# Weight sums of a Strassen down projection: from the down stage to the merge stage, by way of DRAM

## The chip, the cores and the metric

The kernel runs on one core of a Trainium2 chip. A core has five engines that each work through their own list of instructions in order: TensorE (PE, matmuls; PEld is its weight load), VectorE (DVE), ScalarE (ACT), GpSimd (POOL) and SyncE (SP, which here only issues transfers). They wait for each other by semaphores. Transfers are issued by SyncE or GpSimd and done by 16 DMA engines. The metric is the device time of one execution in microseconds; lower is better.

## The reference

A decoder block on x of 1024 tokens by 1024 channels, in float32. Two branches read the same normed input, each is projected to 1024 channels and gated, then follow an output projection and a SwiGLU feed-forward part. What matters here is the merge of the branches and the end:

```python
h = rms_norm(x, norm1_g[l])
z = jnp.einsum('bsd,dn->bsn', h, w_in[l])
...                                    # y_nsa, y_ret: 1024 tokens x 512 each
u = jnp.einsum('nbsc,ncd->bsnd', jnp.stack([y_nsa, y_ret]), w_branch[l])
gates = jax.nn.sigmoid(zm.reshape(b, s, N_BRANCH, D_MODEL))
mixed = jnp.sum(gates * u, axis=2)
x = x + jnp.einsum('bsd,de->bse', mixed, w_out[l])
h = rms_norm(x, norm2_g[l])
ff = jax.nn.silu(h @ ffn_w_gate[l]) * (h @ ffn_w_up[l])     # 1024 x 2816
x = x + ff @ ffn_w_down[l]                                  # w_down: 2816 x 1024
```

## The kernel before

**Products.** A float32 product is made of three passes of TensorE: both operands are split into a high half (ScalarE rounds it to the matmul format) and a low half (VectorE subtracts the high half), and high x high, high x low and low x high are summed in one PSUM bank. So each operand tile costs one ScalarE and one VectorE instruction, `split()`.

**Order.** The Python program doesn't write the engines' lists directly. Generators (streams) yield operations, and a planner (`Sched`, L113 to L208) picks at each step the operation that by its own cost estimates can begin first; for equal begin the priority decides (a lower number first). What it picks is fixed at build time as each engine's order; on the chip an engine never goes past an instruction that waits. An operation given as `Any` (`both()`, L1708) goes to VectorE or GpSimd, whichever the planner expects to end first. Tiles come from rings: `Alloc` takes the next slot of a ring once the one before in it is released.

**The merge stage** (L1228 to L1311). For each of 8 column blocks c there is one branch unit "u" (`w_branch`) and, for c = 0, 1 and 7, two gate units "z" (for c = 2 to 6 the gates were made earlier and come back from `z_scr`). A unit's weights come into `wraw` and are split into `wh`, from a ring of two slots (`hl_ring`, L364). A branch unit is four groups of 12 matmuls, for branch b = 1, 0 and token half 0, 1, each in one of the four PSUM banks "SSSO" (`psS` three times, `psO`). The stream `merge_out` empties a bank: for b = 1 VectorE writes gate x bank into `mx`; for b = 0 it multiplies in place in `sgm` and adds this to `mx`. The branches' outputs y lie in DRAM. `y_loads` brings them in 16 tiles of 128x512 through a ring `yraw` of four slots, and `y_split` splits them into `yt`, in the order b = 1, 0, half 0, 1, k = 0 to 3. Then follow the output projection (`wo`), the norm, and gate and up, which write F in DRAM (`f_scr`).

**The down stage** (L1693 to L1940). F times `w_down` is cut into 2x2 blocks A (of F) and B (of `w_down`), each block into 11 slices k of 128x512 (KH = 11), and done in 7 products instead of 8. With the sums

```
S1 = A21 + A22    S2 = S1 - A11    A22 - A11    A12 - S2
T1 = B12 - B11    T3 = B22 - B12   T2 = B11 + T3    T4 = B21 - T2
```

the products run in the order 2, 1, 5, 6, 3, 7, 4 (`PLAN`, L1698), each as 11 k by 4 row tiles by 3 passes. All 88 sums (8 kinds by 11 k) are made during the stage, by VectorE or GpSimd: `d_s1`, `d_s2` and `d_ops`. Transfers are in pieces of 256 KB: A11, A21, A22, B11, B12 and B22 into tiles that stay, A12 and B21 (twice each) through a ring `st` of six slots. `d_fill` splits an operand into one of the 8 slots of `dop_ring`. The first two k are loaded into old buffers before the last tiles of the gate stage are free ("pool" is not open yet); the rest waits until the pool `f2p` opens. (`wh` in the rows of this stage is one of those old buffers, used as a slot of `dop_ring`.)

Of the kernel before, what the change touches and what calls it, by code (L numbers as in the profile page):

```python
# [16 lines left out]
T = 1024  # L17
# [194 lines left out]
def kernel(  # L212
# [44 lines left out]
    def sb_ring(pool, shape, dt, name, bufs):  # L257
        return Ring([lambda: pool.tile(shape, dt, name=name, bufs=bufs)] * bufs)
# [34 lines left out]
    def tt(o, a, b, op, eng=None):  # L293
        return vop(o, [a, b], lambda: (eng or dve).tensor_tensor(o, a, b, op), eng)  # L294
# [1398 lines left out]

    KH = NF // 2
    LAST = 3
    PLAN = [(2, "V"), (1, "Y"), (5, "V"), (6, "Y"), (3, "V"), (7, "Y"), (4, "V")]  # L1698
    SRC = {1: ("A11", "B11"), 5: ("A21", None), 6: ("A11", "B11"), 3: (None, "B22"), 7: (None, "B12"), 4: ("A22", None)}
# [8 lines left out]
    def both(*a):  # L1708
        return Any(tt(*a, gp), tt(*a))

    def d_of(q, k):

        f, c = (int(q[2]) - 1 if q[0] == "A" else int(q[1]) - 1) * KH + k, int(q[1] if q[0] == "A" else q[2]) - 1
        c = slice(c * 512, c * 512 + 512)
        return f_scr[f][:, c] if q[0] == "A" else ffn_w_down[0][f * 128:(f + 1) * 128, c]

    def st_make(n):
        def make():
            if n < 4:
                return flat(f2["raw"][n // 2])[:, n % 2 * 512:n % 2 * 512 + 512]  # L1720
            return f2["st", n][:, 0:512]
        return make

    def dop_make(n):
        def make():
            if n < 4:
                return flat(f2["hl"][n // 2])[:, n % 2 * 1024:n % 2 * 1024 + 1024].rearrange("p (s t) -> p s t", s=2)
            return f2["op", n][:, 0:2]
# [5 lines left out]
    def d_first():  # L1734
        yield Wait(lambda: n_op[0] == 7 * NF and all((L1, p) in ops for p in (5, 6, 7)))
        f2["raw"] = [(yield Alloc(raw_ring)), (yield Alloc(raw_ring))]
        for k in range(2):
            yield from d_stream(2, k, "A12", gp)
            yield from d_stream(2, k, "B21", gp)
        for n, t in enumerate(fe["h"]):  # L1740
            yield Wait(lambda: n_use[0] >= 7 * NF // 12 * 12 + 2 * n + 2)
            hl_ring.release(t)
        f2["hl"] = [(yield Alloc(hl_ring)), (yield Alloc(hl_ring))]
        yield Wait(lambda: "pool" in f2)
        more = [(q, k) for k in range(KH) for q in ("A11", "B11")]
        more += [(q, k) for k in range(KH) for q in ("A21", "A22", "B12")] + [("B22", k) for k in range(KH)]
        for k in range(2, KH):
            yield from d_stream(2, k, "A12")
            yield from d_stream(2, k, "B21")
            for _ in range(2):  # L1750
                yield from d_quad(*more.pop(0))
        for n, (q, k) in enumerate(more):
            yield from d_quad(q, k)
        for p, q in ((3, "A12"), (4, "B21")):
            for k in range(KH):
                yield from d_stream(p, k, q)
# [18 lines left out]
    def d_s2():  # L1775
        for k in range(KH):
            yield Wait(lambda: ("S1", k) in fl and (1, k, 0) in dop)
# [8 lines left out]
    D_READY = {  # L1786
        (1, 0): lambda k: ("A11", k) in dq, (1, 1): lambda k: ("B11", k) in dq,
        (2, 0): lambda k: ("A12", 2, k) in dq, (2, 1): lambda k: ("B21", 2, k) in dq,
        (5, 0): lambda k: ("S1", k) in fl, (5, 1): lambda k: ("B11", k) in dq and ("B12", k) in dq,
        (6, 0): lambda k: ("S2", k) in fl, (6, 1): lambda k: ("T2", k) in fl,  # L1790
        (3, 0): lambda k: ("A12", 3, k) in dq and ("S2", k) in fl, (3, 1): lambda k: ("B22", k) in dq,
        (7, 0): lambda k: ("S2", k) in fl and ("A22", k) in dq, (7, 1): lambda k: ("T3", k) in fl,
        (4, 0): lambda k: ("A22", k) in dq, (4, 1): lambda k: ("B21", 4, k) in dq and ("T2", k) in fl,
    }

    def d_ops():

        yield Wait(lambda: "hl" in f2)
        for n, (p, k) in enumerate((p, k) for p, _ in PLAN for k in range(KH)):
            if n == 2:  # L1800
                yield Wait(lambda: "pool" in f2)
            for b in range(2):
                yield Wait(lambda: D_READY[p, b](k))
                then = None
                if p == 2 or (p, b) in ((3, 0), (4, 1)):
                    src = dq.pop((("A12", "B21")[b], p, k))
                    then = lambda r=src: st_ring.release(r)
                    if p != 2:
                        yield both(src, src, f2[("A11", "B11")[b], k], ALU.subtract)
                elif (p, b) in ((5, 1), (7, 0)):  # L1810
                    src = yield Alloc(f2["tmp"])
                    then = lambda r=src: f2["tmp"].release(r)
                    x, y = ("B12", "B11") if b else ("A22", "A11")
                    yield both(src, f2[x, k], f2[y, k], ALU.subtract)
                    if b:
                        fl.add(("T1", k))
                else:
                    src = f2[SRC[p][b], k]
                o = yield Alloc(dop_ring)
                sch.spawn(d_fill(p, k, b, o, src, then), 2)  # L1820

# [83 lines left out]
    fe["T"] = sb_ring(fp, [128, 4, 128], F32, "T", 4)  # L1905
    fl.add("fe")
    sch.spawn(s_split(), 1)
    sch.spawn(d_first(), 3)
# [6 lines left out]
    hs.close()  # L1915
    f2p = ctx.enter_context(tc.tile_pool(name="f2p", bufs=1))

    def quads(*names):
        for q, k in names:
            f2[q, k] = f2p.tile([128, 512], F32, name=f"{q}_{k}_")  # L1920

    def d_op(*ns):
        for n in ns:
            f2["op", n] = f2p.tile([128, 2, 512], F32R, name=f"dop{n}")

    every = range(KH)
    quads(*[(q, k) for q in ("A21", "A22") for k in every], *[("B22", k) for k in range(10)])
    d_op(4, 5)
    quads(("B22", 10), *[("B12", k) for k in range(7)])
    d_op(6, 7)  # L1930
    quads(*[("B12", k) for k in range(7, KH)], *[(q, k) for k in every for q in ("A11", "B11")])
    f2["x"] = sb_ring(f2p, [128, 512], F32, "xo", 4)
    f2["x22"] = sb_ring(f2p, [128, 512], F32, "xp", 4)
    for n in (4, 5):
        f2["st", n] = f2p.tile([128, 512], F32, name=f"st{n}")
    f2["tmp"] = sb_ring(f2p, [128, 512], F32, "tmp", 4)
    f2["pool"] = f2p
    sch.spawn(d_s1(), 3)
    sch.spawn(d_s2(), 3)
    sch.spawn(d_x2(), 3)  # L1940
    sch.run()

# [28 lines left out]
```

## Time and profile before

| what | value |
|---|---|
| time, median of 3 runs | 1658.31 us (1657.8 to 1660.41) |
| the profiled execution's own time | 1657.56 us |
| its span in the profile | 1655.8 us |
| mean granted TensorE clock | 0.982 |
| TensorE busy | 1594.2 us, 96% |
| VectorE busy | 1055.4 us, 64% |
| ScalarE busy | 694.9 us, 42% |
| GpSimd busy | 329.0 us, 20% |

The profile is one execution. A view by windows gives each engine's busy time in a stretch and the granted clock of TensorE: 1.00 is the upper of its two levels, 2.4 GHz, 0.50 the lower, 1.2 GHz, and what lies between is a mixture in that window. A timeline gives instructions, or runs of like ones, in order of time; in brackets stands how long the engine was idle before, and what ended the idle time. Names lose their buffer numbers there. Matmuls are pipelined, so the start of the next group says when one is through, better than start plus length.

### The profile page before, as it was taken

What the parts mean: (1) busy time and instruction counts of PE and PEld (TensorE: products, weight loads), DVE (VectorE), ACT (ScalarE), POOL (GpSimd) and SP (SyncE); (2) the same over time, 40 slices, a digit from 0 to 9 for tenths busy, and PEclk for the clock granted to TensorE, in tenths of its full rate; (3) what the DMA queues carried; (4) which work ended last, traced back from release to release, by engine and by line L of the source; (5) the groups of instructions that cost most, each with busy time, mean ns of one, the idle gap of its engine ahead of it and who ended that gap; (6) DMA issues with size and microseconds to landing.
All of it is one profiled execution on the core that took longest, in us unless ns stands there. A gap on an engine that the chain in (4) does not pass through costs nothing.

```text
span 1655.8 us, 23314 instructions
## 1 busy us (share of the span) xinstructions
PE 1594.2 (96%) x8404; PEld 1365.0 (82%) x8404; DVE 1055.4 (64%) x2665; ACT 694.9 (42%) x1410; POOL 329.0 (20%) x338
## 2 busy tenths in 40 slices
PE   7999999999999999999999979999999999897999
PEld 7999888898888888888888867888888888675887
DVE  8566588888789887423447569544444443399785
ACT  5233367665565565132114335333333332332442
POOL 2011212211112120000000025222222220037261
PEclk9999999999999999999999999999999999998999
DMA  6563221211412110233433323222222221872022
GB/s 184 145 189 115 58 65 55 77 30 42 134 57 56 48 49 23 73 110 101 127 127 128 115 89 90 77 89 79 87 90 77 77 77 51 299 306 82 32 90 83
DMA packets 158036, 160.71 MB, mean 97 GB/s; under 512 B 18400, under 2 KB 115680, under 8 KB 157664
## 3 DMA queue, kind: packets, MB, share of 16 engines
q1 hardware_dynamic: 152672, 147.68, 27.9%
q0 software_dynamic: 5248, 11.54, 2.4%
q8 instruction: 66, 1.08, 0.3%
q14 instruction: 50, 0.41, 0.1%
HBM read 120.38 MB, written 38.81 MB: 96 GB/s over the span
## 4 chain that ended last, share of the span: by engine, by line
PE 74%; DVE 6%; DMA 4%; issue 2%; POOL 1%; ACT 1%; SPq 0%; POOLq 0%; DVEq 0%; ACTq 0%
PE psF L264 25%; PE psS L264 22%; PE psO L264 11%; PE psT L264 11%; PE psT L269 4%; DMA wraw<-in_ffn_w_down_dram 1%; DVE P L1011 1%; PE psF L269 1%; DVE P L299 1%; DVE pc L294 0%; DVE wh L294 0%; DMA A__13648<-f_scr 0%; DMA B__13713<-in_ffn_w_down_dram 0%; DMA A__13656<-f_scr 0%; DMA A__13664<-f_scr 0%
## 5 line engine op out<-in xcount | busy, mean ns | idle before, releaser
L264 PE MATMUL psF<-H,wh 128*128 128x512 f32 x1044 | 274.8, 395 | 0.0
L264 PEld LDWEIGHTS psF<-H,wh 128*128 128x128 f32 x1044 | 191.8, 189 | 33.6
L264 PE MATMUL psS<-H,zh 128*128 128x512 f32 x480 | 135.0, 405 | 0.3 <-ACT zs L284 0.3
L284 ACT ACTIVATE P<-P,pm 128x640 f32<-128x640 f32 (+7 forms) x128 | 93.9, 734 | 66.0 <-DVE pm L1011 64.6
L294 DVE TENSOR_TENSOR pT<-psT,pT 128x512 fp32r<-128x512 f32 (+1 forms) x152 | 92.4, 615 | 33.4 <-ACT pT L284 32.8
L284 ACT ACTIVATE pT<-psT 128x512 fp32r<-128x512 f32 (+1 forms) x152 | 78.9, 536 | 70.9 <-PE psT L269 70.4
L264 PE MATMUL psS<-kT,qt 128*128 128x384 f32 (+3 forms) x384 | 103.2, 344 | 2.1 <-DVE pm L1011 2.0
L264 PEld LDWEIGHTS psS<-H,zh 128*128 128x128 f32 x480 | 85.9, 188 | 15.1 <-ACT zs L284 0.6
L264 PE MATMUL psO<-pT,vv 128*128 128x256 f32 x528 | 92.1, 291 | 3.7 <-DVE pT L294 3.6
L284 ACT ACTIVATE wh<-wraw 128x1024 fp32r<-128x1024 f32 (+1 forms) x58 | 48.8, 849 | 99.5 <-PE psO L264 80.1
L264 PEld LDWEIGHTS psO<-pT,vv 128*128 128x128 f32 x528 | 80.1, 191 | 12.6 <-DVE pT L294 5.5
L264 PE MATMUL psS<-whA,H 128*128 128x256 f32 (+1 forms) x672 | 89.1, 290 | 0.0
L294 DVE TENSOR_TENSOR wh<-wraw,wh 128x1024 fp32r<-128x1024 f32 (+1 forms) x58 | 61.2, 1059 | 41.1 <-ACT wh L284 40.9
L264 PEld LDWEIGHTS psS<-whA,H 128*128 128x128 f32 x672 | 85.0, 192 | 0.0
L269 PE MATMUL psT<-ident,P 128*128 128x128 f32 x528 | 80.4, 274 | 0.1
L294 POOL TENSOR_TENSOR sx<-sx 128x512 f32<-128x512 f32 x4 | 5.1, 1282 | 352.0 <-DVE sx L294 352.0
L264 PEld LDWEIGHTS psS<-kT,qt 128*128 128x128 f32 x384 | 65.6, 190 | 10.4 <-DVE pm L1011 2.8
L294 DVE TENSOR_TENSOR op<-T,op 128x512 fp32r<-128x512 f32 x59 | 48.9, 831 | 28.4 <-ACT op L284 28.0
L264 PE MATMUL psS<-yt,wh 128*128 128x512 f32 x288 | 66.6, 389 | 0.0
L269 PEld LDWEIGHTS psT<-ident,P 128*128 128x128 f32 x528 | 62.4, 141 | 4.9 <-DVE P L299 0.8
L264 PE MATMUL psS<-wh 128*128 128x512 f32 x198 | 54.0, 414 | 11.2 <-DVE wh L294 10.1
L264 PE MATMUL psF<-sh,op 128*128 128x512 f32 x264 | 63.7, 390 | 0.7 <-ACT u L284 0.7
(589 smaller groups left out, 3564.9 us busy)
## 6 DMA issues: line engine op xcount, KB each, us to landing
wraw<-in_w_in_dram SPq DMA_DIRECT2D x22, 512.0 KB, 4.1
f_scr<-fs SPq DMA_DIRECT2D x22, 512.0 KB, 2.6
qt<-q_scr POOLq DMA_DIRECT2D x16, 512.0 KB, 4.0
wraw<-in_ffn_w_gate_dram SPq DMA_DIRECT2D x11, 512.0 KB, 3.7
wraw<-in_ffn_w_up_dram SPq DMA_DIRECT2D x11, 512.0 KB, 3.6
xx<-in_ffn_w_gate_dram SPq DMA_DIRECT2D x11, 512.0 KB, 3.7
xx<-in_ffn_w_up_dram SPq DMA_DIRECT2D x11, 512.0 KB, 3.6
rawA<-in_w_in_dram SPq DMA_DIRECT2D x20, 256.0 KB, 3.4
```

Source lines behind the costliest of these rows:

```text
L264: lambda: pe.matmul(o, l, r, start=start, stop=stop, skip_group_check=True))
L269: return Op("pe", 109, 100, [o], [i], lambda: pe.transpose(o, i, ident))
L284: return Op("act", c, 150, outs, ins, lambda: act.activation(o, i, func, scale=scale, **kw))
L294: return vop(o, [a, b], lambda: (eng or dve).tensor_tensor(o, a, b, op), eng)
L299: return vop(o, ins, lambda: (eng or dve).tensor_scalar(o, a, s1, None, op0=op0), eng, fast)
L1011: lambda: dve.tensor_tensor_reduce(o, a, b, -sc, init, ALU.add, ALU.min, acc))
```

## The change

In the merge stage a new stream `wd_sums` (priority 4) loads `w_down` row block by row block (k and KH + k, 128x1024, 512 KB each), forms T1 to T4 in place by four subtractions on VectorE, and stores the two results to new DRAM tiles `t_scr`. All loads and stores are issued by GpSimd: 22 loads and 22 stores. It uses three tiles `row`, of which two take the place of `yraw` as well: the y tiles pass through their halves. It begins when all y tiles are split, and the stage runs until it is done. The pool `big` (with `mx`) moves to the other side of SBUF, and stays open.

In the down stage all B operands (B21, B11, T1, T2, B22, T3, T4, in that order of products) and A12 (twice) pass through one ring `st` of 24 slots; A11, A21 and A22 stay. 44 sums are left: S1, S2, A12 - S2 and A22 - A11, all on VectorE. `dop_ring` has 10 slots, all in old buffers, with the counts `FREE` at which each is free. Eight slots of `st` lie in old buffers, so four k instead of two are loaded, by GpSimd, before the pool opens.

```diff
-    big = es.enter_context(tc.tile_pool(name="big", bufs=1))
+    big = ctx.enter_context(tc.tile_pool(name="big", bufs=1, side="right"))
...
-    yr_ring = sb_ring(yp, [128, 512], F32, "yraw", 4)
+    rows = [yp.tile([128, T], F32, name=f"row{n}") for n in range(3)]
+    yr_ring = Ring([lambda n=n: rows[n // 2][:, n % 2 * 512:n % 2 * 512 + 512] for n in range(4)], True)
...
+    def wd_sums():
+        yield Wait(lambda: all(("yt", b, half, k) in fl for b in range(2) for half in range(2) for k in range(4)))
+        ring = Ring([lambda n=n: rows[n][:, 0:T] for n in (2, 0, 1)], True)
+        nxt = None
+        for k in range(KH):
+            pair = []
+            for i in range(2):
+                if nxt is None:
+                    nxt = yield Alloc(ring)
+                    f = i * KH + k
+                    yield dma(nxt, ffn_w_down[0][f * 128:(f + 1) * 128, :], gp)
+                pair.append(nxt)
+                nxt = None
+            if k + 1 < KH:
+                nxt = yield Alloc(ring)
+                yield dma(nxt, ffn_w_down[0][(k + 1) * 128:(k + 2) * 128, :], gp)
+            a, b, c, d = [r[:, i * 512:i * 512 + 512] for r in pair for i in range(2)]
+            yield tt(a, b, a, ALU.subtract)
+            yield tt(b, d, b, ALU.subtract)
+            yield dma(t_scr[k][0], pair[0], gp)
+            ring.release(pair[0])
+            yield tt(d, d, a, ALU.subtract)
+            yield tt(c, c, d, ALU.subtract)
+            yield dma(t_scr[k][1], pair[1], gp)
+            ring.release(pair[1])
+        fl.add("ts")
...
+    sch.spawn(wd_sums(), 4)
+    sch.run(lambda: "u_done" in fl and "ts" in fl)
...
+    AQ = {1: "A11", 5: "A21", 6: "A11", 4: "A22"}
+    BQ = {2: "B21", 1: "B11", 5: "T1", 6: "T2", 3: "B22", 7: "T3", 4: "T4"}
...
-    st_ring = Ring([st_make(n) for n in range(6)], True)
-    dop_ring = Ring([dop_make(n) for n in range(8)], True)
+    st_ring = Ring([st_make(n) for n in range(NST)], True)
+    dop_ring = Ring([dop_make(n) for n in range(10)], True)
...
+    def d_loads():
+        yield Wait(lambda: ("U", L1) in fl)
+        f2["raw"] = []
+        for k in range(2, KH + 2):
+            if k < 6:
+                r = yield Alloc(raw_ring if k < 4 else fe["raw"])
+                f2["raw"].append(flat(r))
+            elif k == 6:
+                yield Wait(lambda: "pool" in f2)
+            yield from d_stream(2, k - 2, "A12", gp if k < 6 else None)
+            yield from d_stream(2, k - 2, "B21", gp if k < 6 else None)
+        for p, _ in PLAN[1:]:
+            for k in range(KH):
+                for q in {1: ("A11",), 5: ("A21", "A22")}.get(p, ()):
+                    yield dma(f2[q, k], d_of(q, k))
+                    dq[q, k] = f2[q, k]
+                if p == 3:
+                    yield from d_stream(3, k, "A12")
+                yield from d_stream(p, k, BQ[p])
...
+    def d_sums():
         for k in range(KH):
             yield Wait(lambda: ("A21", k) in dq and ("A22", k) in dq)
-            yield both(f2["A21", k], f2["A21", k], f2["A22", k], ALU.add)
+            yield tt(f2["A21", k], f2["A21", k], f2["A22", k], ALU.add)
             fl.add(("S1", k))
...
-            yield both(f2["A11", k], f2["A21", k], f2["A11", k], ALU.subtract)
+            yield Wait(lambda: (1, k, 0) in dop)
+            yield tt(f2["A11", k], f2["A21", k], f2["A11", k], ALU.subtract)
             fl.add(("S2", k))
-            yield Wait(lambda: ("T1", k) in fl and ("B22", k) in dq and (1, k, 1) in dop)
-            yield both(f2["B12", k], f2["B22", k], f2["B12", k], ALU.subtract)
-            fl.add(("T3", k))
-            yield both(f2["B11", k], f2["B12", k], f2["B11", k], ALU.add)
-            fl.add(("T2", k))
...
+    FREE = (144, 144, 146, 146, 148, 148, 152, 152, 154, 154)
...
+                if n < 10:
+                    yield Wait(lambda: n_use[0] >= FREE[n])
+                n += 1
                 o = yield Alloc(dop_ring)
```

The planner's choices move with it. VectorE's list of before, from the low half `wh` of branch unit 4 on; `mx_9006` is the output of column blocks 2 and 3, and the `psS` and `psO` behind it are the four banks of branch unit 2:

```order
L294 TENSOR_TENSOR wh_9430<-wraw_9318,wh_9430 128x1024 [waits DMAHW2_49,PE_49,Activation_49]
L294 TENSOR_TENSOR mx_9006<-psS_9429,sgm_9489 128x512 [waits DMAHW5_49,PE_49]
L294 TENSOR_TENSOR mx_9006<-psS_9449,sgm_9490 128x512 [waits DMAHW6_49,PE_49]
L294 TENSOR_TENSOR sgm_9491<-psS_9463,sgm_9491 128x512 [waits DMAHW7_49,PE_49]
L294 TENSOR_TENSOR mx_9006<-mx_9006,sgm_9491 128x512 [waits DVE_49]
L294 TENSOR_TENSOR sgm_9492<-psO_9476,sgm_9492 128x512 [waits DMAHW0_49,PE_49]
L294 TENSOR_TENSOR wh_9493<-wraw_9381,wh_9493 128x1024 [waits DMAHW3_49,Activation_49]
```

Before, both low halves stand at the ends of the unit's instructions, the one of unit 4 (`wh_9493`) ahead of the last sum only.

VectorE's list of the change in the same place, where `row0`, `row1` and `row2` are the tiles of `wd_sums`:

```order
L294 TENSOR_TENSOR wh_9470<-wraw_9343,wh_9470 128x1024 [waits DMAHW2_49,PE_49,Activation_49]
L294 TENSOR_TENSOR row1_9012<-row1_9012 128x512 [waits DMASW2_49]
L294 TENSOR_TENSOR row1_9012<-row2_9013,row1_9012 128x512 [waits DMASW5_49,DVE_49]
L294 TENSOR_TENSOR row2_9013<-row2_9013,row1_9012 128x512 [waits DVE_49]
L294 TENSOR_TENSOR row2_9013<-row2_9013 128x512 [waits DVE_49]
L294 TENSOR_TENSOR wh_9541<-wraw_9415,wh_9541 128x1024 [waits DMAHW3_49,Activation_49]
L294 TENSOR_TENSOR mx_9006<-psS_9469,sgm_9537 128x512 [waits DMAHW5_49]
L294 TENSOR_TENSOR mx_9006<-psS_9491,sgm_9538 128x512 [waits DMAHW6_49]
L294 TENSOR_TENSOR sgm_9539<-psS_9506,sgm_9539 128x512 [waits DMAHW7_49]
L294 TENSOR_TENSOR sgm_9540<-psO_9521,sgm_9540 128x512 [waits DMAHW0_49]
L294 TENSOR_TENSOR mx_9006<-mx_9006,sgm_9539 128x512 [waits DVE_49]
L294 TENSOR_TENSOR mx_9006<-mx_9006,sgm_9540 128x512 [waits DVE_49]
```

Before, the low half for unit 4 (`wh_9493`) stands behind the third and fourth bank's multiplications; in the change its counterpart, `wh_9541`, stands ahead of the first, and row sums stand between. Further on the same holds for column blocks 3 to 6: `wh` first, then 1, 3, 1 and 1 row sums, then the first `mx`.

SyncE's list of before around the second half of the y loads; `y_scr0` is branch 0:

```order
L318 DMA wraw_9102<-in_w_in_dram 128x8x128 [waits DVE_49]
L318 DMA yraw_9111<-y_scr0_101 128x512 [waits DMAHW3_49,DVE_49]
L318 DMA yraw_9120<-y_scr0_101 128x512 [waits DMAHW4_49,DVE_49]
L318 DMA yraw_9126<-y_scr0_101 128x512 [waits DMAHW5_49,DVE_49]
L318 DMA yraw_9131<-y_scr0_101 128x512 [waits DMAHW6_49,DVE_49]
L318 DMA yraw_9156<-y_scr0_101 128x512 [waits DMAHW0_49,DVE_49]
L318 DMA yraw_9163<-y_scr0_101 128x512 [waits DMAHW1_49,DVE_49]
L318 DMA yraw_9171<-y_scr0_101 128x512 [waits DMAHW2_49,DVE_49]
L318 DMA yraw_9182<-y_scr0_101 128x512 [waits DMAHW7_49,DMAHW3_49,DVE_49]
L318 DMA wraw_9193<-in_w_in_dram 128x8x128 [waits DVE_49]
L318 DMA wraw_9262<-in_w_branch_dram 128x8x128 [waits DVE_49]
```

The loads of `wraw` stand ahead of and behind the eight y loads here.

SyncE's list of the change in the same place:

```order
L318 DMA wraw_9117<-in_w_in_dram 128x8x128 [waits DVE_49]
L318 DMA row1_9012<-y_scr1_102 128x512 [waits DMAHW2_49]
L318 DMA row0_9011<-y_scr0_101 128x512 [waits DMAHW3_49,DVE_49]
L318 DMA row0_9011<-y_scr0_101 128x512 [waits DMAHW4_49,DVE_49]
L318 DMA row1_9012<-y_scr0_101 128x512 [waits DMAHW5_49,DVE_49]
L318 DMA row1_9012<-y_scr0_101 128x512 [waits DMAHW7_49,DVE_49]
L318 DMA wraw_9188<-in_w_in_dram 128x8x128 [waits DVE_49]
L318 DMA row0_9011<-y_scr0_101 128x512 [waits DMAHW0_49,DVE_49]
L318 DMA row0_9011<-y_scr0_101 128x512 [waits DMAHW1_49,DMAHW6_49,DVE_49,Activation_49]
L318 DMA row1_9012<-y_scr0_101 128x512 [waits DMAHW2_49,Activation_49]
L318 DMA row1_9012<-y_scr0_101 128x512 [waits DMAHW3_49,Activation_49]
L318 DMA wraw_9280<-in_w_branch_dram 128x8x128 [waits DVE_49]
```

Before, the second load of gate weights (`wraw_9193`) stands behind all y loads; in the change (`wraw_9188`) it stands ahead of the last four.

VectorE's list of the change in the same place, with the splits of those tiles into `yt0`:

```order
L294 TENSOR_TENSOR wh_9176<-wraw_8868,wh_9176 128x1024 [waits PE_49,Activation_49]
L294 TENSOR_TENSOR yt0_9009<-row0_9011,yt0_9009 128x512 [waits DMAHW0_49,Activation_49]
L294 TENSOR_TENSOR mx_9005<-psS_9175,sgm_9065 128x512 [waits DMASW3_49,DMASW2_49,DMASW6_49,DMASW1_49,DMASW7_49,DMASW0_49,PE_49]
L294 TENSOR_TENSOR mx_9005<-psS_9194,sgm_9101 128x512 [waits PE_49]
L294 TENSOR_TENSOR yt0_9009<-row1_9012,yt0_9009 128x512 [waits DMAHW2_49,Activation_49]
L294 TENSOR_TENSOR yt0_9009<-row1_9012,yt0_9009 128x512 [waits DMAHW3_49,Activation_49]
L294 TENSOR_TENSOR yt0_9009<-row0_9011,yt0_9009 128x512 [waits DMAHW1_49]
L294 TENSOR_TENSOR yt0_9009<-row0_9011,yt0_9009 128x512 [waits DMAHW5_49,Activation_49]
L294 TENSOR_TENSOR sgm_9139<-psS_9219,sgm_9139 128x512 [waits PE_49]
L294 TENSOR_TENSOR mx_9005<-mx_9005,sgm_9139 128x512 [waits DVE_49]
L294 TENSOR_TENSOR yt0_9009<-row0_9011,yt0_9009 128x512 [waits DMAHW6_49,Activation_49]
L294 TENSOR_TENSOR yt0_9009<-row1_9012,yt0_9009 128x512 [waits DMAHW7_49,Activation_49]
```

Before, the last four splits stand together between the first two `mx` of branch unit 0; now one split of the third group stands behind both, and three of the last four behind `sgm_9139`, the product of the third bank.

## Rows read from the trace of the kernel before

**Rows 1.** The page: busy us of each engine, share of the span, instructions.

```profile
PE 1594.2 (96%) x8404; PEld 1365.0 (82%) x8404; DVE 1055.4 (64%) x2665; ACT 694.9 (42%) x1410; POOL 329.0 (20%) x338
```

**Rows 2.** Windows: busy us of each engine; last come clock, DMA share, GB/s.

```profile
729.00:860.00 131.00, 131.00 (x579) 108.45 (x578) 51.52 (x70) 27.25 (x37) 0.00 (x0) 1.00 0.38 119
1412.00:1656.00 244.00, 221.94 (x926) 178.91 (x924) 178.15 (x217) 87.02 (x150) 86.59 (x55) 0.95 0.41 151
```

**Rows 3.** Timeline of TensorE, merge: start, length, engine, line, what; idle in brackets.

```profile
751.46 8.32 PE L264 MATMUL psS<-yt,wh 128*128 128x512 f32 x36
...
803.14 2.88 PE L264 MATMUL psO<-yt,wh 128*128 128x512 f32 x12
805.86 8.32 PE L264 MATMUL psS<-yt,wh 128*128 128x512 f32 x36
```

**Rows 4.** The same, down stage: its first and its last matmuls.

```profile
1412.45 1.98 PE L264 MATMUL psS<-wh 128*128 128x512 f32 x8
...
1651.00 0.84 PE L264 MATMUL psO<-wh 128*128 128x512 f32 x3
```

**Rows 5.** The same: TensorE behind its waits (one is of an earlier stage).

```profile
378.99 0.77 PE L264 MATMUL psF<-rd,re 128*128 128x128 f32 x2 [3.04 <-DVE re L304]
...
1420.96 0.47 PE L264 MATMUL psS<-dop,dop 128*128 128x512 f32 x1 [3.14 <-issue]
...
1443.68 0.50 PE L264 MATMUL psS<-wh 128*128 128x512 f32 x1 [1.04 <-ACT wh L284]
...
1495.16 3.78 PE L264 MATMUL psS<-wh 128*128 128x512 f32 x8 [3.21 <-DVE wh L294]
...
1507.14 3.78 PE L264 MATMUL psS<-wh 128*128 128x512 f32 x8 [6.49 <-DVE wh L294]
```

**Rows 6.** Windows behind those waits, columns as in rows 2.

```profile
379.00:382.00 3.00, 3.00 (x14) 3.00 (x15) 2.19 (x6) 0.00 (x0) 0.00 (x0) 0.50 0.23 85
...
1442.60:1447.00 4.40, 3.14 (x13) 2.17 (x12) 3.10 (x5) 2.71 (x5) 0.00 (x0) 1.00 1.06 407
...
1495.16:1500.60 5.44, 5.44 (x12) 3.81 (x12) 5.44 (x6) 0.71 (x2) 3.35 (x2) 0.50 0.82 262
1507.10:1512.00 4.90, 4.86 (x12) 3.84 (x13) 4.90 (x3) 0.26 (x1) 4.41 (x3) 0.55 0.00 0
```

**Rows 7.** Timelines of VectorE and GpSimd, down stage: sums alone and side by side.

```profile
1489.14 0.68 DVE L294 TENSOR_TENSOR A__13702<-A__13650,A__13702 128x512 f32<-128x512 f32 x1
1489.74 1.77 DVE L294 TENSOR_TENSOR tmp<-B__13685,B__13703 128x512 f32<-128x512 f32 x1
...
1493.73 1.37 DVE L294 TENSOR_TENSOR wh<-tmp,wh 128x512 fp32r<-128x512 f32 x1
...
1489.26 1.71 POOL L294 TENSOR_TENSOR B__13701<-B__13684,B__13701 128x512 f32<-128x512 f32 x1
```

**Rows 8.** Timeline of ScalarE behind a branch unit.

```profile
806.06 1.07 ACT L284 ACTIVATE wh<-wraw 128x1024 fp32r<-128x1024 f32 x1 [9.33 <-PE psO L264]
```

**Rows 9.** Timeline of VectorE around the end of branch unit 2.

```profile
803.28 0.69 DVE L294 TENSOR_TENSOR mx<-psS,sgm 128x512 f32<-128x512 f32 x1 [4.91 <-DMA sgm<-z_scr]
...
807.30 1.21 DVE L294 TENSOR_TENSOR wh<-wraw,wh 128x1024 fp32r<-128x1024 f32 x1
808.43 0.68 DVE L294 TENSOR_TENSOR mx<-mx,sgm 128x512 f32<-128x512 f32 x1
```

**Rows 10.** The same under branch unit 0, and the loads of y.

```profile
753.24 1.23 DVE L294 TENSOR_TENSOR wh<-wraw,wh 128x1024 fp32r<-128x1024 f32 x1 [1.98 <-ACT wh L284]
...
yraw<-y_scr SPq DMA_DIRECT2D x16, 256.0 KB, 3.5
```

**Rows 11.** DMA issues: queue, count, KB each, median us from issue to landing.

```profile
qt<-q_scr POOLq DMA_DIRECT2D x16, 512.0 KB, 4.0
...
vv<-v_scr POOLq DMA_DIRECT2D x2, 512.0 KB, 5.3
...
f_scr<-fs SPq DMA_DIRECT2D x22, 512.0 KB, 2.6
```

More of the change, by code (lines that the diff above doesn't have):

```diff
@@ L1252, in y_split @@
         fl.add(("yt", b, half, k))
+    KH = NF // 2
+    t_scr = [[dram.tile([128, T], F32, name=f"t_scr{k}_{i}") for i in range(2)] for k in range(KH)]
+    def wd_sums():
[24 more added lines that the diff above has]
+        fl.add("ts")
     sg_ring = sb_ring(mw, [128, 512], F32, "sgm", 4)
@@ L1706, in flat @@
         return t.rearrange("p a b n -> p (a b n)") if len(t.shape) == 4 else t.rearrange("p a b -> p (a b)")
-    def both(*a):
-        return Any(tt(*a, gp), tt(*a))
     def d_of(q, k):
+        if q[0] == "T":
+            i, c = {1: (0, 0), 3: (0, 1), 4: (1, 0), 2: (1, 1)}[int(q[1])]
+            return t_scr[k][i][:, c * 512:c * 512 + 512]
         f, c = (int(q[2]) - 1 if q[0] == "A" else int(q[1]) - 1) * KH + k, int(q[1] if q[0] == "A" else q[2]) - 1
@@ L1725, in make @@
         def make():
-            if n < 4:
-                return flat(f2["hl"][n // 2])[:, n % 2 * 1024:n % 2 * 1024 + 1024].rearrange("p (s t) -> p s t", s=2)
-            return f2["op", n][:, 0:2]
-        return make
-    st_ring = Ring([st_make(n) for n in range(6)], True)
-    dop_ring = Ring([dop_make(n) for n in range(8)], True)
[L1734 to L1754, printed above, removed]
-            for k in range(KH):
-                yield from d_stream(p, k, q)
@@ L1779, in d_s2 @@
             fl.add(("S2", k))
[L1780 to L1794 removed]
+    A_HAS = {1: lambda k: ("A11", k) in dq, 5: lambda k: ("S1", k) in fl, 6: lambda k: ("S2", k) in fl,
+             7: lambda k: ("S2", k) in fl, 4: lambda k: ("A22", k) in dq}
@@ L1796, in d_ops @@
+    FREE = (144, 144, 146, 146, 148, 148, 152, 152, 154, 154)
     def d_ops():
[L1798 to L1801, printed above, removed]
+        n = 0
+        for p, k in ((p, k) for p, _ in PLAN for k in range(KH)):
             for b in range(2):
-                yield Wait(lambda: D_READY[p, b](k))
                 then = None
-                if p == 2 or (p, b) in ((3, 0), (4, 1)):
-                    src = dq.pop((("A12", "B21")[b], p, k))
+                if b or p in (2, 3):
+                    q = (BQ[p] if b else "A12", p, k)
+                    yield Wait(lambda: q in dq)
+                    src = dq.pop(q)
@@ L1807, in d_ops @@
                     then = lambda r=src: st_ring.release(r)
[L1808 to L1816, printed above, removed]
-                else:
-                    src = f2[SRC[p][b], k]
+                    if not b and p == 3:
+                        yield tt(src, src, f2["A11", k], ALU.subtract)
+                else:
+                    yield Wait(lambda: A_HAS[p](k))
+                    if p == 7:
+                        src = yield Alloc(f2["tmp"])
+                        then = lambda r=src: f2["tmp"].release(r)
+                        yield tt(src, f2["A22", k], f2["A11", k], ALU.subtract)
+                    else:
+                        src = f2[AQ[p], k]
@@ L1907 @@
     sch.spawn(s_split(), 1)
-    sch.spawn(d_first(), 3)
+    sch.spawn(d_loads(), 3)
     sch.spawn(d_ops(), 3)
@@ L1916 @@
     f2p = ctx.enter_context(tc.tile_pool(name="f2p", bufs=1))
-    def quads(*names):
-        for q, k in names:
+    for n in range(8, NST):
+        f2["st", n] = f2p.tile([128, 512], F32, name=f"st{n}")
+    for q in ("A11", "A21", "A22"):
+        for k in range(KH):
             f2[q, k] = f2p.tile([128, 512], F32, name=f"{q}_{k}_")
[L1922 to L1931, printed above, removed]
     f2["x"] = sb_ring(f2p, [128, 512], F32, "xo", 4)
     f2["x22"] = sb_ring(f2p, [128, 512], F32, "xp", 4)
-    for n in (4, 5):
-        f2["st", n] = f2p.tile([128, 512], F32, name=f"st{n}")
     f2["tmp"] = sb_ring(f2p, [128, 512], F32, "tmp", 4)
     f2["pool"] = f2p
-    sch.spawn(d_s1(), 3)
-    sch.spawn(d_s2(), 3)
+    sch.spawn(d_sums(), 3)
     sch.spawn(d_x2(), 3)
```

17 lines of the change are left out of this document (5 added, 12 removed).

## The prediction

> **What bounds the kernel now.** I read the totals first: TensorE is busy 96% of the span [rows 1], so a change pays or costs only where it removes or makes a wait of TensorE. Two stages are touched, and the busy time by stage sets them apart [rows 2]. From 729 to 860 us, the merge stage, TensorE is busy all of 131.00 us at full clock: nothing can be gained there, and any new wait is paid in full. From 1412 to 1656 us, the down stage, it is busy 221.94 of 244 us at a mean clock of 0.95: there the room lies.
>
> How large is that room? In the merge stage a group of 12 matmuls of 128x512 follows the next after 805.86 - 803.14 = 2.72 us [rows 3], 0.2267 us a matmul. The down stage is 7 products x 11 k x 4 row tiles x 3 = 924 such matmuls, so 209.5 us without a wait. The first one starts at 1412.45 and the last group ends at 1651.00 + 0.84 [rows 4]: 239.4 us. About 30 us are waits and slow clock. Waits are 244 - 221.94 us, less the 4.16 us behind the last matmul, 17.9; the largest stand in the timeline of TensorE, 3.14, 3.21 and 6.49 us [rows 5]. The other 12 us are matmuls at a lowered clock: the granted clock is 0.50 and 0.55 just after the waits of 3.21 and 6.49 us [rows 6], the lower of the two levels (1.2 GHz of 2.4). The first 8 matmuls take 3.78 us after both [rows 5], where 8 take 1.98 at full clock [rows 4]: 1.8 us lost so far. The 5.44 us at 0.50 did the work of 2.72: at most 2.7 us lost. A wait of 3.04 us at 378.99 was followed by 0.50 too, one of 1.04 us at 1443.68 by none (1.00) [rows 5, 6]. Most of these waits end with VectorE, and the engine lines show why: a 128x512 sum on VectorE follows the one before after 0.60 us when alone (1489.14 to 1489.74), but takes 1.77 us while GpSimd does a sum of 1.71 us beside it [rows 7].
>
> **The down stage, what goes.** Of 88 sums, shared by GpSimd and VectorE, 44 stay, all on VectorE; T1 to T4 come out of DRAM ready. GpSimd does no sum there any more, so the 1.7 us forms of VectorE go. VectorE then has 154 low halves, 44 sums and 32 additions of results, 230 x 0.60 = 138 us of work under 209.5 us of matmuls. Four k instead of two of the first product are loaded ahead of the pool, which covers the 3.14 us wait at 1420.96, a wait for transfers. Transfers grow from 110 to 132 pieces of 256 KB. At the 407 GB/s that the stage reached [rows 6] a piece takes 0.64 us; the hungriest product (A21, A22 and T1) needs three, 1.9 us, in the 4 x 3 x 0.2267 = 2.72 us of a k. They stay hidden. I leave 1.9 us for small waits at the start and where the A sums of product 6 first come due: 211.4 us instead of 239.4, **-28**. Bounds: -30 (no wait at all) and -14 (half of the waits return, as stalls on the ring or on VectorE).
>
> **The merge stage, what is added.** The sums are 44 VectorE instructions of 0.60 us, 26 us, on an engine busy 51.52 of 131 us [rows 2]: room enough, if order did not matter. But VectorE works strictly in the order written, and the listing of VectorE's order shows a new one. Before, the four instructions that empty the banks of a branch unit (mx, mx, sgm, ...) stand ahead of the low half `wh` of the weight unit after next; now `wh` stands first, five times, for c = 2 to 6. That `wh` needs ScalarE's high half, which waits for the end of TensorE's unit c, since the weight ring has two slots: ScalarE starts it at 806.06, right after the unit's last group (803.14 + 2.88) [rows 3, 8]. The banks are four, all filled by unit c, so unit c+1 cannot start until `wh` and then the first mx are done. Before, the first mx was done at 803.28 + 0.69, two us ahead of TensorE, and TensorE went on at 805.86 with no wait [rows 3, 9]. After: 805.86 to the start of `wh` 1.44 us (807.30), 1.13 to the next instruction (808.43), mx 0.69, and TensorE starts 0.06 us after VectorE ends (from the wait of 3.21 us, where VectorE's instruction ended at 1493.73 + 1.37 = 1495.10) [rows 5, 7, 9]: 3.32 us a unit. Between `wh` and the first mx stand 0, 1, 3, 1 and 1 row sums as well, 6 x 0.60 = 3.6. So 5 x 3.32 + 3.6 = **+20.2**.
>
> Each of the five is longer than the waits of 3.04 and 3.21 us after which the clock fell [rows 5, 6], so I take a restart at 2.2 us, midway between 1.8 and 2.7: 5 x 2.2 = **+11**. Bounds: 0 (the clock holds) and 13.5.
>
> Unit u0 is late as well. The y tiles now go through the two halves of row0 and row1, and SyncE's listing has the second `wraw` load ahead of the last four y loads. That load waits for VectorE's `wh`, done at 753.24 + 1.23 = 754.47 [rows 10]. VectorE's listing now has three splits of a y tile behind the mx and sgm of u0's own second and third group, which wait for those groups. The second group ends at 751.46 + 2 x 2.72 = 756.9, mx done 0.69 later, then the k = 1 split; the third group thus ends some 2 us late, at about 761.6; its sgm and mx take two steps of 0.6, then three splits, 764.8; the last three matmuls end near 765.9 instead of 762.3: **+3.7**. Bounds: 0 and 7 (y loads take 3.5 us to land [rows 10]).
>
> **The new transfers** are 44 of 512 KB on GpSimd's queue, each row slot loaded, summed and stored. No row shows a store there. The load's nearest row is 4.0 us, its far one 5.3, both on this queue; the store's is 2.6 on SyncE's queue, its far bound 5.3 as well [rows 11]. I take 4.0 and 2.6. A slot's turn, two sums, store, load, with 0.75 us of issue, is 1.2 + 2.6 + 4.0 + 0.75 = 8.6 us for four sums. The order puts about five sums into a branch unit, 10.7 us of transfers against 10.88 + 3.3 + 2.2 + 0.7 = 17 us that a unit then lasts, so it is hidden at nothing. With both at 5.3 the turn is 12.6 and five sums take 15.7, just below 17.
> [...]
>
> GpSimd does nothing else in this stage (0.00 busy [rows 2]), so its queue is theirs. The pool moved to the other side adds nothing that waits; the last waits of the gate stage may shift by +0.5.
>
> **Sum.** 20.2 + 11 + 3.7 - 28 + 0.5 = +7.4 us. The profiled execution has 1657.56 us (span 1655.8), so 1665; the median of the runs shown is 0.75 above it: **1666 us**. The forecast's own range is 1661.7 to 1671.
>
> **Rivals.**
> 1. *The clock holds.* The five waits come, but TensorE goes on at full clock: 20.2 + 3.7 - 28 + 0.5 = -3.6, 1654.7 us, faster. For it: the wait of 1.04 us cost nothing [rows 6]. Against it: three waits of 3.04 to 6.49 us all did. It decides if the waits come out nearer to 1.04 than to 3.04 us; at 2 us each another 5 x 1.3 = 6.6 go, to 1648. The Trainium skill (TensorE: Matmul & The Clock Gate, section "HAM oscillation — how this bites in real kernels") has each such wait restart cold, every time; by it this rival is out, and the rows at 1495 and 1507 agree.
> 2. *The row transfers set the pace.* If a load and a store take 2.6 us more than their rows, the turn is 13.8 us, 17.2 for a unit's five sums, and VectorE waits for a row with mx behind it, in the three-sum place most: I put +3 to +23 on top, 1669 to 1689, about 1676. For it: sums stand between `wh` and mx in four units. Against it: only 38% of the transfer engines' time is used there [rows 2].
> 3. *The down stage keeps half of its waits* (new waits for the ring of 24 slots, or for transfers behind the last f stores): -14 instead of -28, 1680 us. For it: the stage begins with transfers at their limit, 1.06 busy [rows 6]. Against it: demand is at most 1.9 of 2.72 us.
> 4. *The merge stage hides the sums*, as its idle VectorE would suggest; the order's `wh` would have to cost nothing: 3.7 - 28, 1634 us. Against it: two slots and four banks leave TensorE nothing to do meanwhile.
>
> **How the numbers follow.** Forecast 0.52, rival 1 0.17, rival 2 0.13, rival 3 0.12, rival 4 0.06. Within 0.2% (3.3 us, about what a measurement of this kernel can tell from no change) means 1655.0 to 1661.6. Faster: most of rival 1, rival 4 and a small part of the forecast's low end, 0.23. Same: the rest of rival 1 and the forecast's edge, 0.12. Slower: 0.65. The range leaves out rival 4, the low end of rival 1 and the ends of rivals 2 and 3: 1649 to 1682.
>
> **What the profile after would show.** Right: five waits of TensorE of 3.3 to 5.2 us in the merge stage, each ended by VectorE's mx, with a granted clock near 0.5 behind each; the last branch unit ending some 35 us later than before; VectorE's sums in the down stage all near 0.68 us; the down stage about 211 us long with the clock at 1.00. Wrong, if those waits are absent or end with a transfer into row tiles, if the clock stays at 1.00 behind them, or if the down stage shows waits above 1 us, for DMA or for VectorE.

## The result and the profile after

| | median | range |
|---|---|---|
| before | 1658.49 us | 1657.80 to 1660.41, 4 runs |
| the change | 1667.95 us | 1665.04 to 1670.97, 4 runs |

The ratio is 1.0063 (95% interval 1.0037 to 1.0089): slower. The forecast was 1666 us in a range of 1649 to 1682. The profiled execution of the change is the slowest of its four, 1670.97 us (span 1669.3). I compare the profiles by stretches, since the start of the merge stage, ahead of which both programs are the same, lies anywhere between 722 and 731 us in the profiles below.

| stretch | before | change | difference |
|---|---|---|---|
| merge stage, first gate unit to the end of the last branch unit | 130.59 us | 163.59 us | +33.0 |
| from there to the first matmul of the down stage (one is taken in ahead of the rest) | 545.77 us | 551.27 us | +5.5 |
| from there to the last matmul | 245.81 us | 219.46 us | -26.35 |

With 1.4 us of a later start that is 13.5 us, the difference of the two spans.

The timeline of TensorE in the merge stage of the change (start, length, engine, line, what, count, idle time before) answers to [rows 3], where unit follows unit with no wait:

```profile
808.02 2.88 PE L264 MATMUL psO<-yt,wh 128*128 128x512 f32 x12
814.00 10.04 PE L264 MATMUL psS<-yt,wh 128*128 128x512 f32 x36 [3.10 <-DVE mx L294]
823.88 2.88 PE L264 MATMUL psO<-yt,wh 128*128 128x512 f32 x12
830.46 10.86 PE L264 MATMUL psS<-yt,wh 128*128 128x512 f32 x36 [3.70 <-DVE mx L294]
...
849.19 10.01 PE L264 MATMUL psS<-yt,wh 128*128 128x512 f32 x36 [5.15 <-DVE mx L294]
...
865.62 10.02 PE L264 MATMUL psS<-yt,wh 128*128 128x512 f32 x36 [3.70 <-DVE mx L294]
...
882.05 10.06 PE L264 MATMUL psS<-yt,wh 128*128 128x512 f32 x36 [3.70 <-DVE mx L294]
```

There are five waits, each ended by VectorE's `mx`, with 0, 1, 3, 1 and 1 row sums between `wh` and `mx`. Behind each the three groups that take 8.32 us at full clock [rows 3] take 10.0 to 10.9. Windows of TensorE behind the first two waits (busy us, then clock, DMA share, GB/s) show the granted clock that does it, and its return to the upper level:

```profile
814.00:819.00 5.00, 5.00 (x15) 0.66 1.00 353
830.40:836.00 5.60, 5.54 (x14) 0.53 0.99 319
820.00:824.00 4.00, 4.00 (x19) 1.00 0.71 276
```

VectorE's timeline at the first wait answers to [rows 9]: `wh` first, released by ScalarE, and `mx` behind it.

```profile
812.03 1.23 DVE L294 TENSOR_TENSOR wh<-wraw,wh 128x1024 fp32r<-128x1024 f32 x1 [1.97 <-ACT wh L284]
813.17 1.28 DVE L294 TENSOR_TENSOR mx<-psS,sgm 128x512 f32<-128x512 f32 x2
```

By stage (columns as in [rows 2]) the merge stage has 147.09 of 169 us busy where it had all; the down stage is at full clock, GpSimd idle:

```profile
729.00:898.00 169.00, 147.09 (x601) 118.30 (x600) 80.31 (x116) 29.17 (x39) 23.61 (x44) 0.94 0.68 232
1440.00:1669.00 229.00, 222.78 (x975) 182.34 (x973) 142.76 (x228) 87.82 (x151) 0.00 (x0) 1.00 0.52 184
```

Of its waits one above 1.1 us is left, 13.7 us into product 6 (which begins at 1543.05), against those of [rows 5]; its VectorE instructions take 0.68 to 0.69 us, none the 1.77 of [rows 7]:

```profile
1558.69 1.43 PE L264 MATMUL psF<-op 128*128 128x512 f32 x5 [1.59 <-DVE op L294]
```

The new transfers (DMA issues of the whole span, columns as in [rows 11]) took 4.3 and 3.6 us, where I had 4.0 and 2.6; no run shows why the stores are slower than those of [rows 11]:

```profile
row<-in_ffn_w_down_dram POOLq DMA_DIRECT2D x22, 512.0 KB, 4.3
...
t_scr<-row POOLq DMA_DIRECT2D x22, 512.0 KB, 3.6
```

### The profile page after: what moved, and what is told of

It is laid out like the page before. It is cut to its first block, busy times and chain, and to the rows that moved or that the text cites. A ratio compares the mean times of both kernels' runs of the same rounds, so it can differ in the third digit from the quotient of the medians.

```text
span 1669.3 us, 23475 instructions
## 1 busy us (share of the span) xinstructions
PE 1601.4 (96%) x8404; PEld 1365.7 (82%) x8404; DVE 1041.6 (62%) x2720; ACT 695.8 (42%) x1410; POOL 268.9 (16%) x331
## 4 chain that ended last, share of the span: by engine, by line
PE 80%; DVE 5%; issue 1%; ACT 1%; DMA 1%; POOL 0%; DVEq 0%; ACTq 0%; POOLq 0%
PE psF L264 26%; PE psS L264 25%; PE psO L264 12%; PE psT L264 12%; PE psT L269 4%; DVE P L1011 1%; PE psF L269 1%; DVE P L299 1%; DVE pc L294 0%; DMA row<-y_scr 0%; ACT wh L284 0%; DVE wh L294 0%; DVE pT L294 0%; DVE sh L294 0%; POOL T L294 0%
## 5 line engine op out<-in xcount | busy, mean ns | idle before, releaser
L264 PE MATMUL psS<-yt,wh 128*128 128x512 f32 x288 | 76.3, 428 | 20.8 <-DVE mx L294 19.3
L284 ACT ACTIVATE wh<-wraw 128x1024 fp32r<-128x1024 f32 (+1 forms) x49 | 43.3, 889 | 114.7 <-PE psO L264 99.3
L264 PEld LDWEIGHTS psS<-yt,wh 128*128 128x128 f32 x288 | 60.0, 210 | 36.6 <-issue 21.3
L294 DVE TENSOR_TENSOR wh<-wraw,wh 128x1024 fp32r<-128x1024 f32 (+1 forms) x49 | 52.4, 1069 | 54.3 <-ACT wh L284 54.2
L264 PE MATMUL psS<-wo,H 128*128 128x512 f32 x216 | 62.1, 392 | 0.0
```

Of the source, the lines that this page charges most:

```text
L264: lambda: pe.matmul(o, l, r, start=start, stop=stop, skip_group_check=True))
L284: return Op("act", c, 150, outs, ins, lambda: act.activation(o, i, func, scale=scale, **kw))
```

## Experiments

The theory: the order of VectorE in the merge stage costs 33 us, the down stage gives 27. Rivals: the 23 MB of transfers slow the merge stage; the changes depend on each other. Open besides: the 5.5 us in the stretch between. Each kernel was timed beside the kernel before on the same chip.

**change_again** (no edit)

> The changed kernel once more, for a second profile. In the first one 6.2 us were lost between the end of the merge stage and the first matmul of the down stage (558.4 us against 552.2), where matmuls follow each other about 1% slower at a granted clock of 1.00; the forecast had put 0.5 us there. Theory A (that run was a slow one of its kind: its time 1670.97 is 3 us above the median): this stretch takes 552 to 555 us here, and the time is 1665 to 1668. Theory B (the change itself does it, by where its tiles now lie): 557 to 559 us again. Both: five waits of 3 to 5 us in the merge stage, stage +33, down stage 211 to 213 us.

Measured: 1664.45 against 1655.58 us, ratio 1.0062 (1.0037 to 1.0086). Merge stage 163.93, stretch between 551.29, down 219.49: all three repeat within 0.4 us. Theory A falls: the 5.5 us belong to the change.

**down_only** (part of the edit; `wd_sums` itself goes too)

```diff
-    sch.spawn(wd_sums(), 4)
...
-            return t_scr[k][i][:, c * 512:c * 512 + 512]
+            return ffn_w_down[0][(i * KH + k) * 128:(i * KH + k + 1) * 128, c * 512:c * 512 + 512]
```

> The change without wd_sums: no row loads, sums or stores in the merge stage, y tiles through their own ring as before, and the operands T1 to T4 of the down stage are read straight from blocks of w_down in the same sizes (so its products are made with other numbers). Theory (the down stage gives 27 us, the merge stage costs 33): merge stage 131 us as before, down stage 211 to 213 us, time 1631 to 1634, plus up to 6 if theory B on the stretch between holds (1637). Rival (the down stage's gain comes partly from data that lay ready, or the merge loss is not from wd_sums): above 1645.

Measured: 1633.45 against 1655.58 us, ratio 0.9864 (0.9847 to 0.9882). Merge stage 130.59 to the hundredth, stretch between 551.28, down 219.50. The loss comes with `wd_sums`. The gain is there without it, though this kernel leaves the sums T1 to T4 out, so that its products are not those of the reference.

**merge_only** (the kernel before, with the `rows` and `wd_sums` of the change)

> The kernel before with wd_sums in its merge stage and the y tiles through its row tiles; the down stage is the one before and makes its sums itself, the stored sums are not read. Theory: five waits of 3 to 5 us in the merge stage, 33 us longer, down stage 239 us as before: 1689 to 1693. Rival (most of the loss comes with the moved pool or the other down stage): under 1680. This kernel keeps the pool where it was, so theory B on the stretch between expects 552 us there, and its time is then 1691.

Measured: 1687.40 against 1655.58 us, ratio 1.0194 (1.0172 to 1.0215). Merge stage 160.94, stretch between 545.78, down 244.66. The time is a little under the 1689 to 1693 expected, but its runs spread from 1680 to 1690 us, and the profile is of the fastest; by stretches the parts add up. The stretch between is as before where the pool `big` stays on the left. The merge stage is 2.65 us shorter than in the change, nearly all of it by the clock: its first wait is the same, but TensorE went on at full speed, 8.44 us for three groups (the change: 10.04):

```profile
805.22 8.44 PE L264 MATMUL psS<-yt,wh 128*128 128x512 f32 x36 [3.10 <-DVE mx L294]
```

**order_fixed**

```diff
+            if id(u) in after_mx:
+                yield Wait(lambda: ("m1", after_mx[id(u)]) in fl)
             hl = yield Alloc((u.ring() if callable(u.ring) else u.ring) or hl_ring)
...
+    after_mx = {id(b_units[c + 2]): c for c in range(2, 6)}
+    after_mx[id(m_units[7][1])] = 6
...
+            if half == 1:
+                fl.add(("m1", c))
```

> The changed kernel with one rule more: the split of the weight unit that takes unit c's slot (c = 2 to 6) is written only after the two first multiplications (mx) of unit c. All loads, sums and stores stay, so does the ring of three row tiles. Theory (the place of wh ahead of mx costs 20 us of waits and 9 of slow clock): those five waits end otherwise or are gone; the y loads' 3.5 us stay. If the row transfers hide, 1668 - 29 = 1639. But with units of 10.9 us instead of 16.5 about six sums stand in a unit, 1.5 turns of some 9.4 us (load 4.4, store 3.6, two sums): 14 us, so I expect VectorE to wait for rows with mx behind it, some 5 to 20 us in all: 1644 to 1658. Rival (transfers, not the order, slow the merge stage): 1664 or more.

Measured: 1666.65 against 1655.58 us, ratio 1.0065 (1.0050 to 1.0080); merge stage 159.6 us. A miss, outside the 1644 to 1658 expected: 4 us were won of the 29 that the order was to give. The time alone would fit the rival (1664 or more); only paced tells the two apart. The first of the five waits is gone, and one of 8.82 us stands at the next unit. VectorE's timeline shows its cause:

```profile
818.30 1.42 DVE L294 TENSOR_TENSOR row<-row,row 128x512 f32<-128x512 f32 x2 [4.80 <-DMA row<-in_ffn_w_down_dram]
819.75 1.29 DVE L294 TENSOR_TENSOR row<-row 128x512 f32<-128x512 f32 x2
826.50 0.69 DVE L294 TENSOR_TENSOR row<-row,row 128x512 f32<-128x512 f32 x1 [5.45 <-DMA row<-in_ffn_w_down_dram]
827.10 0.68 DVE L294 TENSOR_TENSOR mx<-psS,sgm 128x512 f32<-128x512 f32 x1
```

VectorE waits for the row of the next k, and the ready `mx` is queued behind it: rival 2 of the forecast, which the five waits had hidden. From 805.08 to 873.96 six turns, each from a sum that needs the second row of one k to that of the next, take 68.9 us, 11.5 each, more than a unit's 10.88.

**paced** (order_fixed, the delayed weight splits on VectorE alone, the y loads in the order of before, 32 bytes of padding, and)

```diff
+        pace = {5: 2, 6: 3, 7: 4, 8: 6}
...
+            if k in pace:
+                yield Wait(lambda: all(("mix", pace[k], half) in fl for half in range(2)))
             yield tt(a, b, a, ALU.subtract)
```

> Three repairs on the change at once: the weight split of unit c+2 written after the first two mx of unit c (as in order_fixed), the row sums of k = 5, 6, 7 and 8 written only after all mx of unit 2, 3, 4 and 6, so that a late row has no mx behind it within the unit, and the planner told that the two halves of a row tile are apart, which puts the y loads back in the order of before; and the 32 bytes of padding. All transfers and sums stay. Theory (waits of TensorE come from what stands behind a waiting VectorE instruction, not from the traffic): u0 without its 3.5 us, at most small waits (a turn of 10 to 11.5 us a k against 10.9 us a unit), merge stage 131 to 137 us instead of 163.6; with the stretch between at 545.8 the time is 1655.6 + 0 to 6 - 27 = 1629 to 1635. Rival (transfers of 23 MB slow the merge stage wherever the sums stand): merge stage 145 us or more, 1643 or more.

Measured: 1645.80 against 1655.85 us, ratio 0.9940 (0.9922 to 0.9959): faster than both. Merge stage 135.67 us with all transfers and sums still in it, u0 without its loss. So the traffic as such costs little, at most the 5 us that the merge stage is still longer than before; what stands behind a waiting VectorE instruction costs. But the stretch between grew to 558.1 us, with TensorE waiting for `wo`, whose tiles take the room of the row tiles, so the time missed the 1629 to 1635 expected. It would fit the rival (1643 or more); the merge stage, which the rival put at 145 us or more, doesn't.

**pool_move** (the kernel before with one line changed)

```diff
-    big = es.enter_context(tc.tile_pool(name="big", bufs=1))
+    big = es.enter_context(tc.tile_pool(name="big", bufs=1, side="right"))
```

> The kernel before with one line changed: the pool big (mx, later the op tiles of the gate stage) on the right side of SBUF, as in the change, and nothing else. In the change the stretch from the merge stage's end to the down stage takes 551.3 us in three runs of it, 545.8 in the kernels with big on the left; matmuls whose moving operand is an op tile follow each other after 0.229 to 0.233 us there instead of 0.224 to 0.227, those on wh tiles do not differ. Theory B (the place of the tiles does it): this stretch takes 551.3 us here too, merge and down stage as before, time +5.5, about 1661. Rival (something in the other changes, such as the transfers or the order of the gate stage): 545.8 us, no difference.

Measured: 1660.95 against 1655.85 us, ratio 1.0031 (1.0013 to 1.0049); merge stage 130.59, stretch between 551.32. Theory B holds: the place of the pool alone costs the 5.5 us. Two such groups of 12 matmuls on `op` tiles, first in the kernel before, where they start 2.72 us apart, then in pool_move, 2.80 apart:

```profile
1204.75 2.88 PE L264 MATMUL psT<-sh,op 128*128 128x512 f32 x12
1207.47 2.88 PE L264 MATMUL psO<-sh,op 128*128 128x512 f32 x12
...
1206.01 2.96 PE L264 MATMUL psT<-sh,op 128*128 128x512 f32 x12
1208.81 2.96 PE L264 MATMUL psO<-sh,op 128*128 128x512 f32 x12
```

**right_padded** (32 bytes ahead of `big`)

> The changed kernel with an unused tile of 32 bytes a partition allocated on the right ahead of big. The mx and op tiles then begin at byte 196544 and so on, a multiple of 64, instead of 196576, a multiple of 32 only; before they began at 110336, a multiple of 64. Theory C (the start address modulo 64 makes the op operand slower to read): the stretch between is 545.8 us again, the down stage, whose operands lie in such tiles too, 1 to 2 us shorter, time 6 to 8 us under the change run beside it (1664.45 on the last chip), about 1657. Rival (it is the far end of SBUF, or the side): 551.3 us again, 1664.

Measured: 1664.57 against 1655.85 us, ratio 1.0051 (1.0033 to 1.0070); stretch between 547.58, groups on `op` mostly 2.91 us. The stretch answers in part, 3.7 us of the 5.5; the time, against 1664.45 in change_again, does not.

**pad_96**

> The changed kernel with 96 bytes of padding on the right instead of 32, so the mx and op tiles begin at multiples of 128 (196480) and not only of 64 (196544). So far 12 matmuls on an op tile take 2.88 us with the pool on the left (110336, a multiple of 256), 2.96 at 196576 (of 32), mostly 2.91 at 196544 (of 64). If the address modulo 128 is what counts: 2.88 here, the stretch between 545.8 us instead of 547.6. If 64 was enough and the side does the rest: 2.91 and 547.6 again. Time 1656 to 1663; merge stage 161 to 164 as in the change.

Measured: 1665.30 against 1654.32 us, ratio 1.0055 (1.0034 to 1.0075); stretch between 551.28, groups on `op` 2.94 to 2.96. Neither outcome came: a multiple of 128 is no better than one of 32, so modulo 128 falls, and the time is above the 1656 to 1663 expected too.

**dve_only** (the kernel before, `both()` without GpSimd)

```diff
-        return Any(tt(*a, gp), tt(*a))
+        return tt(*a)
```

> The kernel before with one line changed: both() gives all 88 sums of the down stage to VectorE, GpSimd does none. Nothing is moved to the merge stage. It tells apart why the down stage waits: theory D (a VectorE instruction takes 1.77 us beside a GpSimd sum and 0.68 alone; that is what starves TensorE): all VectorE instructions of the stage near 0.68, 274 of them x 0.60 = 164 us under 209.5 us of matmuls, most waits of the stage gone except the first one for transfers and some in product 5, where five sums and two low halves a k (7 x 0.60 = 4.2 us) stand against 2.72 us of matmuls; down part (from the end of the gate stage) 226 to 236 us instead of 245.8, time 1636 to 1647 with the kernel before at 1655.8. Rival (the number of sums is the limit, so half of them must go): longer than before, 1660 or more.

Measured: 1648.44 against 1654.32 us, ratio 0.9967 (0.9950 to 0.9984). Down part 235.89 us, 10 less, VectorE's instructions at 0.69. Theory D holds for these 10 us of the 26 in the profile. The time missed its range of 1636 to 1647: the median fell by 5.9 us (2.6 to 8.3), less than the stage did in the one execution profiled. The first wait, for transfers (3.43 us), and one in product 5 stay:

```profile
1411.08 1.98 PE L264 MATMUL psS<-wh 128*128 128x512 f32 x8
...
1419.88 4.13 PE L264 MATMUL psS<-dop,dop 128*128 128x512 f32 x9 [3.43 <-issue]
...
1452.10 1.52 PE L264 MATMUL psF<-dop,dop 128*128 128x512 f32 x6
...
1492.09 3.53 PE L264 MATMUL psS<-wh 128*128 128x512 f32 x8 [4.24 <-DVE wh L294]
```

From line to line the first product (2) takes 1452.10 - 1411.08 = 41.0 us here. In the kernel before it takes 43.1, and in the change 29.85:

```profile
1453.05 2.00 PE L264 MATMUL psS<-op 128*128 128x512 f32 x8
...
1482.90 1.54 PE L264 MATMUL psF<-wh 128*128 128x512 f32 x6
```

Product 5 takes 45.2 us before, 37.2 here and 30.1 in the change. So taking the sums from GpSimd pays in product 5 above all, and what the change gains beyond that lies in products 2 (11.2 us) and 5 (7.2 us).

**paced2** (pace = {5: 2, 6: 3, 7: 4, 8: 5, 9: 6}, 96 bytes)

> paced with two things changed. Its merge stage was 135.7 us, but the output projection behind it waited (the stretch between 558.1 us), since the last row sums (k = 9, 10) and their stores ended some 10 us later, and the wo tiles take the room of the row tiles. Here the sums of k = 8 and 9 follow the mx of unit 5 and 6 (not both of unit 6), and the padding is 96 bytes. If the late rows were what delayed wo: the stretch between falls to 546 to 552 us, the merge stage stays 134 to 139, time 1645.8 - 6 to - 12 = 1634 to 1640 beside 1655.8 for the kernel before. Rival (the rows' transfers cannot end earlier, a turn of 10 to 11.5 us a k is their limit): the waits move into the merge stage again, sum of both stretches unchanged at 693 us, 1644 or more.

Measured: 1641.00 against 1654.32 us, ratio 0.9906 (0.9884 to 0.9927). Merge stage 135.41, stretch between 552.68: the late rows had delayed `wo`. Of what is left there, the padding of 96 bytes has its 5.5, as in pad_96; the time is 1 us above the 1634 to 1640 expected.

**paced2_224** (224 bytes)

> paced2 with 224 bytes of padding instead of 96: three of the four op tiles begin at 204544, 212736 and 220928, multiples of 256, and so all four as in the kernel before (there 118528, 126720, 134912 and 220928, all multiples of 256; one of them lay at the far end and its groups took 2.88 us as the others). In the change the fourth (188160, a multiple of 256) is the one whose groups take 2.88. Theory C' (the start modulo 256 counts): all groups of 12 on op tiles 2.88 us, the stretch between 547 us instead of 552.7, time 5 to 6 us under paced2, 1634 to 1637 beside 1654.3 for the kernel before. Rival (something else about the right side): 2.95 again, 552.7 us, 1641.

Measured: 1635.76 against 1655.62 us, ratio 0.9889 (0.9871 to 0.9907), the best of all. Groups on `op` take 2.88 us again, 85 of 87 (the other two stand behind a wait):

```profile
1211.72 2.88 PE L264 MATMUL psT<-sh,op 128*128 128x512 f32 x12
1214.44 2.88 PE L264 MATMUL psO<-sh,op 128*128 128x512 f32 x12
```

The stretch between is 549.2 us, 2 more than expected, with waits for `wo` of 0.5 to 0.8 us in it; the merge stage 133.33.

## Why the prediction was right

- **Waits of the merge stage**, +20.2: the units' starts, against a start right after the unit before, come late by 3.25, 3.86, 5.31, 3.86 and 3.86, together 20.1. The forecast read this number from the order of the lists and rows of before alone.
- **Slow clock**, +11: 9.4 (1.7 to 2.5 a unit). The bound of 0 was not idle: the first of the five waits, 3.10 us in each profile that has all five, was followed by 10.03 or 10.04 us for three groups in the change, change_again and pad_96, but by 8.44 and 8.43 in merge_only and right_padded. In paced full clock stayed after 2.22 and 2.33 us, in paced2 it fell after 2.19. What decides between these stays open. The Trainium skill (TensorE: Matmul & The Clock Gate, section "HAM oscillation — how this bites in real kernels") describes a kernel that starts cold after every single wait of about 3 to 5 us. The waits of 3.7 us and more in these merge stages agree, those of 3.10 us only in part.
- **u0**, +3.7: 14.33 us instead of 10.88, +3.45. paced, with the y loads in their old order, has 10.88; order_fixed, with the new order, has not.
- **Down stage**, -28: -27.0 between the ends that the forecast used (239.4 to 212.35 us), -26.4 in the table, whose stretch begins one matmul earlier. The size was right, the mechanism named too narrowly: "most of these waits end with VectorE" holds for product 5 (45.2 us before), and GpSimd's sums account for 10 us (dve_only). The largest single part, 11 us of the other 16, is product 2, which waited for transfers, directly and through ScalarE; the forecast saw only its wait of 3.14 us. The change loads four k of it ahead, and no longer loads A11 and B11 between its operands; no run separates the two.
- **The rest**, +0.5: +5.5. This is the step that failed, "the pool moved to the other side adds nothing that waits": nothing waits, but matmuls became slower, and the forecast had put that at nothing. The misses here (5.0 us) and in the down stage (1.6) make the change slower, the smaller terms for the clock (1.6) and u0 (0.25) offset some of it: by stretches the sum is +12.2 instead of +7.4, while the medians differ by 9.5. That the time came within 2 us of 1666 is in part luck.
- Rival 4 fell with the five waits, rival 1 with the slow clock behind them, rival 3 with the down part. Rival 2 did not decide here (no row was late ahead of an `mx`), but was next: with the order repaired it took 25 of the 29 us back.

## What to carry to other kernels

Work moved onto an idle engine costs by its place in that engine's order: compare the order of before and after around each buffer that the busiest engine waits for, and price what stands ahead of the instruction that frees it. When such a wait is repaired, look for the one behind it; an instruction that waits for a transfer belongs behind everything that is ready, not ahead of it. And when a pool moves, compare the duration of one group of matmuls on its tiles.

## What was not expected of the hardware

A matmul's pace depended on where its `op` operand lies in SBUF. The granted clock was 1.00 in all stretches compared. The traces show no addresses; those here are worked out from the program's allocation. Groups of 12 took 2.88 us where the tile's start was a multiple of 256 bytes (the kernel before, paced2_224). They took mostly 2.96 at a start 224 bytes above such a multiple (the change), 2.94 to 2.96 at 128 above (pad_96), and mostly 2.91 at 192 above (right_padded). One of the aligned tiles lay at 220928, near the far end, so the end itself isn't slow. With one such offset tried for each of the three, this is no rule for others; why 192 is better than 128 stays open, and no run separated the start of the tile from its distance to the other operands.
